# Decay tables in smaller portions, states' products a step later, values a step later with four buffers, new rows transposed twelve steps later: one layer of a hybrid transformer

## The chip, the core and the metric

The kernel runs on one core of one Trainium2 chip. The metric is the time of one execution on the device in microseconds (us); lower is better. PE is TensorE (matrix products and transposes), DVE VectorE, ACT ScalarE, POOL GpSimd, and SP the engine that issues most of the transfers.

## What is computed

One layer on a sequence of 2048 rows of width 1024, with 256 context rows beside it. Cut to what matters here:

```
h  = modulate(rmsnorm(x), sh1, sc1);  hc = modulate(rmsnorm(ctx), csh1, csc1)
rq, rk, rv, rg, aq, ak, av = split(h @ w_in)       # retention q, k, v, gate; attention q, k, v
log_gamma = log1p(-exp(ret_log_rate))
s_f = final state of the context's rk, rv          # and s_b, backward
ret = retention(rq, rk, rv, log_gamma, s_f) + the same backward, normed, gated with rg
att = softmax(q k^T / 8) v                         # 8 heads, 2 kv heads, keys of rows and context
x  = x + g1 * (concat(ret, att) @ w_out)
h2 = modulate(rmsnorm(x), sh2, sc2)
x  = x + g2 * (square(relu(h2 @ w_ff1)) @ w_ff2)
out = rmsnorm(x) * final_norm_g
```

Retention works in chunks of 128 rows: a state (128 x 128 for each of 4 heads) is multiplied by a decay and gets k^T v of the chunk added, with k weighted by powers of gamma. The decays come from `log_gamma`, by a series.

## The kernel before

The order of all work is written out by hand; nothing is rearranged by a scheduler. Each engine executes its own queue in that order, and semaphores make it wait for what it needs.

**Stage 1, to about 647 us: projections.** The rows stand in three groups of 6 tiles of 128 rows. For each group and each of six column groups of `w_in` (RK, AKV, AQ, RQ, RV, RG; 512 columns wide, AKV 256) there are six units, one for each tile. A unit is 24 matmuls (L1063 to L1065): eight slices of 128 of the width, in three products of high and low halves of fp32. A column group's weights come in four quarters: a transfer (L506, SP), the high half (L512, ACT), the low half (L516, DVE). All other work hangs on the unit's number: `do(s, part, fn)` puts `fn` behind the products of unit s, and `run_step` (L307) runs the parts in the order hi, evac, turned, low, vec, pool, root, aux, turn, load, store. The AKV column of the second group has units 30 to 35, AQ 36 to 41, RK 42 to 47, then RQ, RV, RG; of the third group AKV has 66 to 71, AQ 72 to 77, RK 78 to 83.

Three pieces of that other work are changed:

- `decay_tables(34)` (L936 to L1012) loads the rates; ACT makes u = exp(rate) in unit s + 2; DVE makes the series of log(1 - u) in s + 3 (22 instructions of 128x8, L955 to L967), ACT the plain logarithm in s + 4, DVE the choice between both in s + 5 (`choose`, 4 instructions, L974 to L977), four times two instructions of 128x128 in s + 6 (`power`, L982 and L983), ACT the exponentials in s + 7, DVE the diagonal in s + 8.
- `forward_state(45 + 3c, c)` (L1016 to L1052) for twelve chunks c: SP loads k and v (L1024) into two slots of 512 in the buffer `early`; POOL weighs k one unit later (L1027); PE makes four products of 128x128 a unit after that (L1032, tile psf; a row of the trace counts x8, since each is issued in two passes); DVE updates the state (L1038, L1040), and SP stores it (L1045).
- `value_parts(82)` (L751 on) loads the attention's values and splits them for the products.

Transposes of keys and queries stand in the units too (L744 for attention's keys, L618 for the others); they use a ring of two banks (psx), which DVE or ACT frees by a copy (L749, the keys' copy; L692).

**Stage 2, about 647 to 1612 us: attention, with retention and the output projection woven in.** `on(k, phase, fn)` puts work in step k; in a step the phases run in the order begin, scores, piece, maximum, early, exp, cast, low, chain, pe, values, late, dma. 32 groups (16 tiles of rows, 2 kv heads) have 18 steps each. A step holds for one key tile two score matmuls (L209, L210), and for the next group one piece (L172), a product whose maximum DVE takes (L185, nm) as the softmax's shift. Behind: exp (L215, ACT, into p32, a ring of three pairs of key tiles), cast to the high half phi (L219, ACT), the low half plo (L226 on POOL for the pairs 0, 2, 4, 6, 7; L228 on DVE for the others) and, every second step, `values` (L242, L243): 16 products of plo and phi with the values. `combine` (L261, POOL, tile ma) ends a group. `retention(24)` (from L1391) makes the backward states and the chunks' output in steps that follow one another every 35 (L1417: state products; L1441: scores). `output_weights(20)` loads the output weights, POOL scales them (L1555, wos), ACT and DVE split them (L1560). `output_tile` (L1568 to L1682) multiplies a finished tile with them: transposes of retention's and attention's rows (L1588), 16 places of products (L1603 to L1605), residual, sum of squares, `norm` on POOL (L1630, tile xr); then, at k + 27 and k + 28, `transpose_x` (L1635, PE, into a bank), one step later `modulate` (L1640, DVE, tile u) and `shift_` (L1645, POOL), and `store_h`. `h_pair` (L1686 to L1716) combines two such tiles on POOL for the feed-forward part, in steps that begin when the tile is finished (the step that `output_tile` returns). `more_keys` (L1306 to L1310) copies keys for the second kv head.

**Stage 3, to 2815 us: the feed-forward part**, by seven products in place of eight, then the last norm.

Of the kernel before, what the change touches and what calls it, by code (L numbers as in the profile page):

```python
# [13 lines left out]
F16 = mybir.dt.float16  # L14
# [3 lines left out]
ALU = mybir.AluOpType  # L18
# [4 lines left out]
P = 128  # L23
# [33 lines left out]
def layer_kernel(ctx: ExitStack, tc: tile.TileContext, a: dict, out: bass.AP):  # L57
# [89 lines left out]
    class Group:  # L147
# [69 lines left out]
        def cast(self, j):  # L217
            hi = self.hi[j] = pp.tile([P, 2, 512], F16, name="phi", tag="phi")
            nc.scalar.activation(hi, self.p[j], AF.Copy)  # L219

        def low(self, j, i=None):
            if i in (None, 0):
                self.lo[j] = pp.tile([P, 2, 512], F16, name="plo", tag="plo")
# [43 lines left out]
    with ExitStack() as st, tc.manual_schedule():  # L267
# [671 lines left out]
        def decay_tables(s):  # L939
# [15 lines left out]
            def series():  # L955
                u, w1, z, zz, lg = (x[v] for v in ("u", "w1", "z", "zz", "lg"))
                nc.vector.tensor_scalar(w1, u, -1.0, 1.0, op0=ALU.mult, op1=ALU.add)
                nc.vector.tensor_scalar(z, u, -1.0, 2.0, op0=ALU.mult, op1=ALU.add)
                nc.vector.reciprocal(z, z)
                nc.vector.tensor_mul(z, z, u)  # L960
                nc.vector.tensor_mul(zz, z, z)
                nc.vector.tensor_scalar(lg, zz, 1.0 / 17, 1.0 / 15, op0=ALU.mult, op1=ALU.add)
                for k in range(13, 0, -2):
                    nc.vector.tensor_mul(lg, lg, zz)
                    nc.vector.tensor_scalar_add(lg, lg, 1.0 / k)
                nc.vector.tensor_mul(lg, lg, z)
                nc.vector.tensor_scalar_mul(lg, lg, -2.0)  # L967
# [38 lines left out]
            do(s + 3, "aux", series)  # L1006
            do(s + 4, "hi", log)
            do(s + 5, "aux", choose)
            for h in range(4):
                do(s + 6, "aux", power, h)  # L1010
                do(s + 7, "hi", tables, h)
            do(s + 7, "hi", rest)  # L1012
            do(s + 8, "aux", diagonal)
# [3 lines left out]
        def forward_state(s, c):  # L1017

            k, v = (early[:, 512 * i : 512 * i + 512].rearrange("p (h d) -> p h d", h=4) for i in range(2))
            st = early[:, 1536:2048].rearrange("p (h d) -> p h d", h=4)  # L1020

            def load():
                for to, src in ((k, rk_d[c]), (v, rv_d[c])):
                    nc.sync.dma_start(to.rearrange("p h d -> p (h d)"), src)  # L1024
# [22 lines left out]
            do(s, "load", load)  # L1047
            do(s + 1, "pool", weigh)
            do(s + 2, "turn", product)
            do(s + 3, "vec", update)  # L1050
            if c > 0:
                do(s + 4, "store", keep_state)  # L1052
# [83 lines left out]
        value_parts(first[2, C_RK] + 4)  # L1136
        decay_tables(first[1, C_AKV] + 4)
# [1093 lines left out]
```

## Time and profile before

| | |
|---|---|
| median of 3 runs | 2817.0 us (2816.18 to 2820.16) |
| profiled execution: its time, its span | 2816.61 us, 2814.7 us |
| mean granted TensorE clock | 0.989 |
| bytes moved | 482.88 MB, 172 GB/s in the mean |
| share of the chain that ended last: PE, DVE, POOL | 57%, 6%, 5% |

The share of an engine is its busy time by the span. "PEld" is the loading of PE's stationary operand, which overlaps its products. In a list of waits, "PE o L242 <- POOL plo L226: 18.4, 15, 2.5" reads: before its line 242 (which writes tile o), PE waited for POOL's line 226 (which writes plo), 18.4 us in 15 waits, 2.5 the longest. In rows by time, the first two numbers are start and duration in us, then engine, line, operation, output and inputs, shapes; in brackets stands how long the engine was idle before it and for whom. Rows of windows give for each stretch its length and the busy time of each engine (with the number of instructions), the granted clock, the DMA engines' busy share and GB/s.

### The profile page before, as it was taken

How to read it: one execution, taken by the hardware profiler on the slowest of the kernel's cores; microseconds unless marked ns; L12 is line 12 of the kernel's file. 1: busy time of each engine (PE TensorE's matmuls, PEld its weight loads, DVE VectorE, ACT ScalarE, POOL GpSimd, SP SyncE). 2: the span in 40 equal slices, each digit the busy share in tenths (PEclk: the TensorE clock that was granted, in tenths of full speed). 3: DMA queues.
4: the chain of work that ended last, by engine and by line, in shares of the span. 5: the costliest groups of instructions: out<-in, count | busy, mean ns of one | idle time of the engine just before them, and what ended most of it. 6: DMA issues, size and time to landing. Idle time of an engine off the chain costs nothing.

```text
span 2814.7 us, 46065 instructions
## 1 busy us (share of the span) xinstructions
PE 2668.3 (95%) x16756; PEld 1602.8 (57%) x16756; DVE 2190.4 (78%) x3126; ACT 1465.0 (52%) x2441; POOL 1933.2 (69%) x1499
## 2 busy tenths in 40 slices
PE   6998999997899999999999899999999999999996
PEld 3877788875566566555666544444444444444443
DVE  3678847777977787877877578898876688888898
ACT  2535443335777777777777745555544322222232
POOL 2527427434766668886766679988865688888887
PEclk9999999999999999999999999999999999999998
DMA  6776876855211223333121264777783757575543
GB/s 213 269 260 203 283 274 218 283 180 184 66 52 52 66 72 106 96 105 91 60 82 45 91 236 138 234 252 248 245 275 106 249 180 284 176 274 171 187 143 112
DMA packets 329778, 482.88 MB, mean 172 GB/s; under 512 B 81991, under 2 KB 192839, under 8 KB 325070
## 3 DMA queue, kind: packets, MB, share of 16 engines
q1 hardware_dynamic: 329166, 479.66, 51.7%
q8 instruction: 132, 2.16, 0.3%
q14 instruction: 96, 0.79, 0.1%
q10 hardware_dynamic: 384, 0.26, 0.0%
HBM read 327.64 MB, written 152.20 MB: 170 GB/s over the span
## 4 chain that ended last, share of the span: by engine, by line
PE 57%; DVE 6%; POOL 5%; issue 2%; DMA 2%; ACT 1%; SPq 0%; POOLq 0%; DVEq 0%; ACTq 0%
PE pu L1838 7%; PE pu L1839 7%; PE pu L1837 7%; PE pd L2056 5%; PE pd L2054 5%; PE pd L2055 5%; PE o L243 3%; PE st L210 3%; PE st L209 3%; PE mp L172 3%; PE o L242 2%; PE bank L1603 2%; PE bank L1605 2%; PE bank L1604 2%; POOL plo L226 1%
## 5 line engine op out<-in xcount | busy, mean ns | idle before, releaser
L185 DVE TENSOR_REDUCE nm<-mp 128x1 f32<-128x512 f32 (+1 forms) x576 | 390.1, 684 | 170.9 <-PE mp L172 144.7
L226 POOL TENSOR_TENSOR plo<-p,phi 128x1024 f16<-128x1024 f32 x160 | 354.1, 2214 | 175.3 <-ACT phi L219 148.0
L215 ACT ACTIVATE p<-st 128x512 f32<-128x512 f32 x576 | 338.5, 597 | 196.8 <-PE st L210 128.2
L2056 PE MATMUL pd<-w,uf 128*128 128x512 f16 x896 | 339.6, 379 | 1.2 <-DVE uf L2047 1.2
L1837 PE MATMUL pu<-hf,w1f 128*128 128x512 f16 x896 | 339.6, 379 | 0.0
L1838 PE MATMUL pu<-hf,w1f 128*128 128x512 f16 x896 | 339.6, 379 | 0.0
L1839 PE MATMUL pu<-hf,w1f 128*128 128x512 f16 x896 | 339.6, 379 | 0.0
L2054 PE MATMUL pd<-w,uf 128*128 128x512 f16 x896 | 339.6, 379 | 0.0
L2055 PE MATMUL pd<-w,uf 128*128 128x512 f16 x896 | 339.6, 379 | 0.0
L219 ACT ACTIVATE phi<-p 128x1024 f16<-128x1024 f32 x288 | 303.9, 1055 | 0.0
L1065 PE MATMUL pso<-whi,hlo_l 128*128 128x512 f32 (+1 forms) x768 | 288.5, 376 | 10.6 <-DVE hlo_l L492 10.5
L1063 PE MATMUL pso<-whi,hhi_l 128*128 128x512 f32 (+1 forms) x768 | 297.5, 387 | 0.8 <-ACT whi L512 0.8
L1064 PE MATMUL pso<-wlo,hhi_l 128*128 128x512 f32 (+1 forms) x768 | 286.8, 373 | 0.8 <-DVE wlo L516 0.8
L242 PE MATMUL o<-wv,plo 128*128 128x65 f16 x2304 | 234.7, 193 | 25.2 <-POOL plo L226 18.4
L228 DVE TENSOR_TENSOR plo<-p,phi 128x512 f16<-128x512 f32 x256 | 241.2, 943 | 19.5 <-ACT phi L219 14.4
L2094 POOL TENSOR_TENSOR d<-d,g2b 128x512 f32<-128x512 f32 x126 | 199.8, 1586 | 70.5 <-DVE d L2066 68.6
L242 PEld LDWEIGHTS <-plo 128*128 128x128 f16 x2304 | 206.3, 98 | 68.6 <-POOL plo L226 26.4
L243 PE MATMUL o<-wv,phi 128*128 128x129 f16 x2304 | 242.5, 220 | 0.0
L1854 POOL TENSOR_TENSOR r<-r 128x512 f32<-128x512 f32 x128 | 172.1, 1350 | 86.4 <-ACT r L1853 86.1
L209 PE MATMUL st<-qr,ks 128*128 128x512 f16 x576 | 220.6, 383 | 7.0 <-ACT p L215 6.6
L210 PE MATMUL st<-qr,ks 128*128 128x512 f16 x576 | 220.7, 383 | 0.4
L172 PE MATMUL mp<-ks,qr 128*128 128x512 f16 x512 | 196.8, 384 | 25.6 <-DVE nm L185 25.2
(330 smaller groups left out, 6249.1 us busy)
## 6 DMA issues: line engine op xcount, KB each, us to landing
wm<-in_w_ff SPq DMA_DIRECT2D x64, 512.0 KB, 6.9
u<-r SPq DMA_DIRECT2D x128, 256.0 KB, 4.6
ur<-u SPq DMA_DIRECT2D x128, 256.0 KB, 5.9
y<-x SPq DMA_DIRECT2D x64, 512.0 KB, 6.4
wst<-in_w_in SPq DMA_DIRECT2D x60, 512.0 KB, 6.8
wf<-w2f SPq DMA_DIRECT2D x112, 256.0 KB, 3.9
w<-wf SPq DMA_DIRECT2D x28, 1024.0 KB, 10.1
w1r<-in_w_ff SPq DMA_DIRECT2D x48, 512.0 KB, 5.3
```

The source lines that it names most:

```text
L185: nc.vector.tensor_reduce(dst, src, axis=AX.X, op=ALU.max, negate=True)
L210: mm(ps, ks2[:, self.g, k], q[:, 1], start=False, stop=True)
L215: nc.scalar.activation(self.p[kt // 2][:, kt % 2], self.s.pop(kt), AF.Exp, scale=HD**-0.5)
L226: nc.gpsimd.tensor_tensor(lo, p, hi, op=ALU.subtract)
L242: mm(o[:, : HD + 1], lo[:, i, c], v[:, : HD + 1], start=False, stop=False)
L243: mm(o, hi[:, i, c], v[:, :VW], start=False, stop=last)
L1837: mm(pu[hf, i], whi, hi, start=k == 0, stop=False)
L1838: mm(pu[hf, i], whi, lo, start=False, stop=False)
L1839: mm(pu[hf, i], wlo, hi, start=False, stop=k == 3)
L2054: mm(ps, u[:, 0, b], w[:, b, 0], start=b == 0, stop=False)
L2055: mm(ps, u[:, 0, b], w[:, b, 1], start=False, stop=False)
L2056: mm(ps, u[:, 1, b], w[:, b, 0], start=False, stop=b == 3)
```

## The change

1. `phi` and `plo` get four buffers in place of three, `values` comes one step later (k + 2j + 7), a group's end likewise, and what follows attention (`prelude`) one step later.
2. The decay series runs in three portions in units s + 3 to s + 5, `choose` moves to s + 6, `power` to s + 7 and s + 8 (two heads each), the tables to s + 8 and s + 9, the diagonal to s + 10; the whole begins one unit later.
3. In `forward_state` the loads rotate over three slots; k is loaded one unit earlier, v in the same unit as before; the product comes two units behind the weighting in place of one, the update and the store follow. The slot of v for chunk c + 1 is that of k of chunk c, so that its load waits for the product of chunk c.
4. `value_parts` begins two units later.
5. `transpose_x` moves from k + 27 and k + 28 to k + 39 and k + 41 (not for tile 1 and the last one), and all that hangs on it with it: modulate, shift, stores, and the steps of `h_pair`.
6. `retention` begins four steps later, and `more_keys(1)` moves from steps 26, 30, 34 to 30, 33, 36.

```diff
--- before.py
+++ after.py
@@ -215,12 +215,12 @@
             nc.scalar.activation(self.p[kt // 2][:, kt % 2], self.s.pop(kt), AF.Exp, scale=HD**-0.5)
 
         def cast(self, j):
-            hi = self.hi[j] = pp.tile([P, 2, 512], F16, name="phi", tag="phi")
+            hi = self.hi[j] = pp.tile([P, 2, 512], F16, name="phi", tag="phi", bufs=4)
             nc.scalar.activation(hi, self.p[j], AF.Copy)
 
         def low(self, j, i=None):
             if i in (None, 0):
-                self.lo[j] = pp.tile([P, 2, 512], F16, name="plo", tag="plo")
+                self.lo[j] = pp.tile([P, 2, 512], F16, name="plo", tag="plo", bufs=4)
             lo, p, hi = self.lo[j], self.p[j], self.hi[j]
             if i is None:
                 nc.gpsimd.tensor_tensor(lo, p, hi, op=ALU.subtract)
@@ -952,19 +952,21 @@
             def base():
                 nc.scalar.activation(x["u"], x["lr"], AF.Exp)
 
-            def series():
+            def series(i):
                 u, w1, z, zz, lg = (x[v] for v in ("u", "w1", "z", "zz", "lg"))
-                nc.vector.tensor_scalar(w1, u, -1.0, 1.0, op0=ALU.mult, op1=ALU.add)
-                nc.vector.tensor_scalar(z, u, -1.0, 2.0, op0=ALU.mult, op1=ALU.add)
-                nc.vector.reciprocal(z, z)
-                nc.vector.tensor_mul(z, z, u)
-                nc.vector.tensor_mul(zz, z, z)
-                nc.vector.tensor_scalar(lg, zz, 1.0 / 17, 1.0 / 15, op0=ALU.mult, op1=ALU.add)
-                for k in range(13, 0, -2):
+                if i == 0:
+                    nc.vector.tensor_scalar(w1, u, -1.0, 1.0, op0=ALU.mult, op1=ALU.add)
+                    nc.vector.tensor_scalar(z, u, -1.0, 2.0, op0=ALU.mult, op1=ALU.add)
+                    nc.vector.reciprocal(z, z)
+                    nc.vector.tensor_mul(z, z, u)
+                    nc.vector.tensor_mul(zz, z, z)
+                    nc.vector.tensor_scalar(lg, zz, 1.0 / 17, 1.0 / 15, op0=ALU.mult, op1=ALU.add)
+                for k in ((13, 11), (9, 7, 5), (3, 1))[i]:
                     nc.vector.tensor_mul(lg, lg, zz)
                     nc.vector.tensor_scalar_add(lg, lg, 1.0 / k)
-                nc.vector.tensor_mul(lg, lg, z)
-                nc.vector.tensor_scalar_mul(lg, lg, -2.0)
+                if i == 2:
+                    nc.vector.tensor_mul(lg, lg, z)
+                    nc.vector.tensor_scalar_mul(lg, lg, -2.0)
 
             def log():
                 nc.scalar.activation(x["ln"], x["w1"], AF.Ln)
@@ -1003,25 +1005,27 @@
 
             do(s, "load", load)
             do(s + 2, "hi", base)
-            do(s + 3, "aux", series)
-            do(s + 4, "hi", log)
-            do(s + 5, "aux", choose)
+            for i in range(3):
+                do(s + 3 + i, "aux", series, i)
+            do(s + 5, "hi", log)
+            do(s + 6, "aux", choose)
             for h in range(4):
-                do(s + 6, "aux", power, h)
-                do(s + 7, "hi", tables, h)
-            do(s + 7, "hi", rest)
-            do(s + 8, "aux", diagonal)
+                do(s + 7 + h // 2, "aux", power, h)
+                do(s + 8 + h // 2, "hi", tables, h)
+            do(s + 8, "hi", rest)
+            do(s + 10, "aux", diagonal)
 
         states = {}
 
         def forward_state(s, c):
 
-            k, v = (early[:, 512 * i : 512 * i + 512].rearrange("p (h d) -> p h d", h=4) for i in range(2))
-            st = early[:, 1536:2048].rearrange("p (h d) -> p h d", h=4)
-
-            def load():
-                for to, src in ((k, rk_d[c]), (v, rv_d[c])):
-                    nc.sync.dma_start(to.rearrange("p h d -> p (h d)"), src)
+            k, v, st = (
+                early[:, 512 * i : 512 * i + 512].rearrange("p (h d) -> p h d", h=4)
+                for i in (2 * c % 3, (2 * c + 1) % 3, 3)
+            )
+
+            def load(to, src):
+                nc.sync.dma_start(to.rearrange("p h d -> p (h d)"), src)
 
             def weigh():
                 nc.gpsimd.tensor_tensor(k, k, bc(kd[:, 0].unsqueeze(2), [P, 4, P]), op=ALU.mult)
@@ -1044,12 +1048,13 @@
             def keep_state():
                 nc.sync.dma_start(sf_d[c - 1], st.rearrange("p h d -> p (h d)"))
 
-            do(s, "load", load)
+            do(s - 1 if c else s, "load", load, k, rk_d[c])
+            do(s, "load", load, v, rv_d[c])
             do(s + 1, "pool", weigh)
-            do(s + 2, "turn", product)
-            do(s + 3, "vec", update)
+            do(s + 3, "turn", product)
+            do(s + 4, "vec", update)
             if c > 0:
-                do(s + 4, "store", keep_state)
+                do(s + 5, "store", keep_state)
 
         AKV, AQ, RK, RV, RQ, RG = (
             (C_AKV, 256), (C_AQ, 512), (C_RK, 512), (C_RV, 512), (C_RQ, 512), (C_RG, 512)
@@ -1133,8 +1138,8 @@
         at += slots((1, C_RK, range(6)), (1, C_RQ, range(6)), (2, C_AQ, range(6)), (2, C_RK, range(3)))
         for i in range(32, 72):
             magnitude_of(i, at.pop(0))
-        value_parts(first[2, C_RK] + 4)
-        decay_tables(first[1, C_AKV] + 4)
+        value_parts(first[2, C_RK] + 6)
+        decay_tables(first[1, C_AKV] + 5)
         for c in range(STATES):
             forward_state(first[1, C_RK] + 3 + 3 * c, c)
         ff_scales(first[2, C_RV] - 3)
@@ -1369,12 +1374,12 @@
                 else:
                     for i in range(2):
                         on(k + 2 * j + 4 + i, "low", g.low, j, i)
-                on(k + 2 * j + 6, "values", g.values, j)
-            k += NK + 5
+                on(k + 2 * j + 7, "values", g.values, j)
+            k += NK + 6
             on(k, "cast", g.evacuate)
             on(k + 1, "chain", g.invert)
             on(k + 2, "late", g.combine, ats)
-        return NK * len(groups) + LAG + 8
+        return NK * len(groups) + LAG + 9
 
 
 
@@ -1672,7 +1677,7 @@
                 rest.extend([(f, q) for f in (transpose_x, modulate, shift_, store_h)])
             return made, made + 5
         for q in range(2):
-            at = k + (31 if t == 1 else 27) + q
+            at = k + (31 + q if t == 1 else 39 + 2 * q)
             on(at, "pe", transpose_x, q)
             on(at + 1, "early", modulate, q)
             on(at + 1, "late", shift_, q)
@@ -1718,9 +1723,9 @@
 
     for i in range(3):
         on(18 + i, "begin", more_keys, 0, i)
-        on(26 + 4 * i, "late", more_keys, 1, i)
+        on(30 + 3 * i, "late", more_keys, 1, i)
     done = attention()
-    retention(24)
+    retention(28)
     output_weights(20)
     for n, t in enumerate(range(NT - 1, -1, -1)):
         made_at, last = output_tile(t, R0 + 43 + RF * n, n == NT - 1)
```

The lines of the changed kernel are up to 5 higher (L1032 is L1036 there, L1635 is L1640). Three places in the order of instructions:

On DVE, around the keys' copy L749 that follows `power`, with the small instructions of the decay tables (tile early), the modulation's accumulation (macc) and the weights' low halves (wlo). Before:

```order
L378 SCALAR_TENSOR_TENSOR macc<-wmo,cc,macc 128x512 x2
L982 TENSOR_SCALAR early<-early 128x128
L983 SCALAR_TENSOR_TENSOR early<-early 128x128
...
L516 TENSOR_TENSOR wlo<-wst,whi 128x1024 x3
L749 CAST ks<-psx 128x2x128
L692 TENSOR_TENSOR qhl<-psx,qhl 128x512
```

And with the change:

```order
L378 SCALAR_TENSOR_TENSOR macc<-wmo,cc,macc 128x512 x2
L965 TENSOR_TENSOR early<-early 128x8
L966 TENSOR_SCALAR early<-early 128x8
...
L968 TENSOR_TENSOR early<-early 128x8
L969 TENSOR_SCALAR early<-early 128x8
L516 TENSOR_TENSOR wlo<-wst,whi 128x1024 x3
L749 CAST ks<-psx 128x2x128
L692 TENSOR_TENSOR qhl<-psx,qhl 128x512
```

Where four pairs of L982 and L983 on 128x128 stood ahead of the copy, the last three pairs of the series on 128x8 stand now; `choose` follows one unit later, and `power` in the two units behind that, ahead of copies of queries (L692).

On PE, at the eighth of the states' products (psf), with the units' products around it (pso; the numbers in hhi_l and hlo_l name the tile). Before:

```order
L1063 MATMUL pso<-whi,hhi_l_4449 128x256
L1064 MATMUL pso<-wlo,hhi_l_4449 128x256
L1065 MATMUL pso<-whi,hlo_l_4450 128x256
L1032 MATMUL psf<-early 128x128 x4
L1063 MATMUL pso<-whi,hhi_l_4509 128x256
L1064 MATMUL pso<-wlo,hhi_l_4509 128x256
```

And with the change:

```order
L1068 MATMUL pso<-whi,hhi_l_4509 128x256
L1069 MATMUL pso<-wlo,hhi_l_4509 128x256
L1070 MATMUL pso<-whi,hlo_l_4510 128x256
L1036 MATMUL psf<-early 128x128 x4
L1068 MATMUL pso<-whi,hhi_l_4571 128x256
L1069 MATMUL pso<-wlo,hhi_l_4571 128x256
```

The product stands one unit later, behind the products of tile 4509 instead of ahead of them.

On PE in attention, at the transposes of a tile's new rows (L1635 before, L1640 after; xr is the row tile that POOL's `norm` leaves), with scores (st), pieces (mp) and values (o) around. Before:

```order
L172 MATMUL mp<-ks,qr 128x512
L1441 MATMUL bank_9793<-oqt,okt 128x128 x4
L1635 MATMUL bank_9798<-ident,xr 128x128 x4
L209 LDWEIGHTS ks
L209 MATMUL st<-qr,ks 128x512
...
L1635 MATMUL bank_9815<-ident,xr 128x128 x4
L242 LDWEIGHTS plo
L242 MATMUL o_9440<-wv,plo 128x65
```

And with the change:

```order
L209 MATMUL st<-qr,ks 128x512
L210 LDWEIGHTS ks_6684
L210 MATMUL st<-qr,ks_6684 128x512
L196 MATMUL mp<-ident,mt_6691 128x128 x4
L172 LDWEIGHTS qr
L172 MATMUL mp<-ks,qr 128x512
L1640 MATMUL bank_10084<-ident,xr 128x128 x4
L242 LDWEIGHTS plo
L242 MATMUL o_9875<-wv,plo 128x65
```

Before, the two halves of a tile stood in neighbouring steps, the first beside a retention score product; now each stands in a step with values, twelve and thirteen steps later.

## Prediction

> **What bounds the kernel now.** I read the profile from the whole to the place: busy shares, then stretches, then who waits for whom, then the rows at each wait that the change touches.
>
> ```profile
> span 2814.7 us, 46065 instructions
> PE 2668.3 (95%) x16756; PEld 1602.8 (57%) x16756; DVE 2190.4 (78%) x3126; ACT 1465.0 (52%) x2441; POOL 1933.2 (69%) x1499
> ```
>
> ```profile
> core 0: us, PE busy (x) PEld busy (x) DVE busy (x) ACT busy (x) POOL busy (x), PEclk, DMA share, GB/s
> 0.00:640.00 640.00, 599.11 (x3065) 481.74 (x3066) 446.53 (x753) 260.16 (x465) 289.24 (x335) 0.99 0.71 241
> 640.00:780.00 140.00, 109.02 (x943) 74.42 (x942) 120.44 (x191) 91.25 (x146) 88.37 (x59) 0.94 0.39 121
> 780.00:1610.00 830.00, 781.96 (x7283) 511.89 (x7282) 634.09 (x1103) 631.97 (x1035) 573.55 (x428) 0.99 0.25 74
> 1610.00:2770.00 1160.00, 1154.68 (x5369) 524.79 (x5367) 952.67 (x1038) 469.83 (x769) 951.47 (x651) 1.00 0.64 213
> ```
>
> TensorE (PE) is busy 95% of the span. The change leaves its work as it is (the same products and transposes), so it can only return or add idle time. The feed-forward stretch (1610 to 2770) has 5 us of idle PE and nothing of the change in it but its entrance; projections, retention and attention have 41, 31 and 48 us. Whom PE waits for there, in the list of waits (total, times, longest, in us):
>
> ```profile
> PE mp L172 <- DVE nm L185: 25.2, 34, 2.2
> PE o L242 <- POOL plo L226: 18.4, 15, 2.5
> PE bank L1635 <- POOL xr L1630: 7.1, 8, 2.4
> PE o L242 <- DVE plo L228: 6.7, 11, 1.8
> PE st L209 <- ACT p L215: 6.6, 8, 3.4
> PE psx L744 <- DVE ks L749: 6.4, 2, 6.0
> PE psx L618 <- DVE ks L749: 1.0, 1, 1.0
> PE bank L1588 <- DVE u L1640: 3.9, 10, 0.8
> PE bank L1588 <- POOL ma L261: 2.9, 1, 2.9
> PE bank L1635 <- DVE u L1640: 1.1, 2, 0.7
> ```
>
> Each part of the change meets one of these rows, or one of three waits shown below. So the question for each is what becomes late next. I work with the profiled execution, which took 2816.61 us (1.9 outside its span); the median of the three runs is 0.4 above it.
>
> **A. Decay tables in smaller portions.** On VectorE (DVE) around 280 us:
>
> ```profile
> 268.44 0.17 DVE L974 TENSOR_SCALAR early<-early 128x8 f32<-128x8 f32 x1
> 269.01 1.22 DVE L516 TENSOR_TENSOR wlo<-wst,whi 128x1024 fp32r<-128x1024 f32 x1
> 275.86 0.28 DVE L982 TENSOR_SCALAR early<-early 128x128 f32<-128x128 f32 x1
> 279.49 3.49 DVE L516 TENSOR_TENSOR wlo<-wst,whi 128x1024 fp32r<-128x1024 f32 x3
> 282.90 0.42 DVE L749 CAST ks<-psx 128x256 f16<-128x256 f32 x1
> 283.46 0.66 PE L744 MATMUL psx<-ident,kn 128*128 128x128 f32 x2 [6.00 <-DVE ks L749]
> 284.80 0.78 PE L1063 MATMUL pso<-whi,hhi_l 128*128 128x512 f32 x1
> 286.76 0.39 PE L1065 MATMUL pso<-whi,hlo_l 128*128 128x512 f32 x1
> ```
>
> PE waits 6.00 us for L749, the copy that frees a transposes' bank; DVE comes to it at 282.90, out of a backlog. Ahead of it the change takes out the eight instructions of `power` (275.86 to 279.49: 3.63 us) and the four of `choose` (268.44 to 269.01: 0.57), which go one step later, `power` in two portions. The 22 small instructions of the series (0.17 us each by the first row, 3.7 in all) stay ahead, in three portions. So L749 comes 3.63 + 0.57 = **4.2 us** earlier, less than the 6.00, and all of it is PE's gain if the moved portions meet no wait in the units behind, where the list names none of theirs. Bounds: 0 (the series' portions or `power` delay the next copy) and 7.0 (the 6.00, and 1.0 that a transpose of L618 waits for the same line).
>
> Does the clock come back too? The matmul at 284.80 takes 0.78 us and that at 286.76 takes 0.39, so a few behind the wait ran slowly, about 1.2 us together. The wait that stays is about 2 us, and waits of about that length were followed by a lower clock elsewhere (2.77 us at 453, 2.53 at 1159):
>
> ```profile
> 450.00:460.00 10.00, 7.24 (x48) 7.03 (x47) 8.49 (x17) 4.28 (x10) 9.51 (x13) 0.83 0.47 143
> 1160.00:1170.00 10.00, 9.70 (x77) 7.13 (x76) 5.85 (x9) 6.36 (x10) 10.00 (x8) 0.83 0.30 74
> ```
>
> I count no clock gain. [...]
>
> **B. States' products two steps behind the weighting.**
>
> ```profile
> 453.04 1.57 PE L1032 MATMUL psf<-early 128*128 128x128 f32 x8 [2.77 <-POOL early L1027]
> 458.98 0.60 SPq L506 DMA_DIRECT2D wst<-in_w_in  x1
> 464.20 1.05 PE L1032 MATMUL psf<-early 128*128 128x128 f32 x8
> 465.78 1.41 DVE L516 TENSOR_TENSOR wlo<-wst,whi 128x1024 fp32r<-128x1024 f32 x1 [1.22 <-ACT whi L512]
> ```
>
> One product of twelve waits, 2.77 us, in the narrow column: the two products stand three narrow units apart, 11.2 us with the first, so a narrow unit is 3.2 us and a wide one 6.4. A step later POOL has long weighted, and the wait goes. Late next is the last quarter of the following column's weights: its low halves are ready at 465.78 + 1.41 = 467.2. PE needs them 18 of 24 matmuls (4.0 us at 0.22, the distance of full-speed matmuls in the rows under D) into the unit that starts at 464.20 + 1.05 = 465.2, at 469.2. PE can come 2.0 us earlier before it waits there. The product of 464.20, which moves out of the stretch ahead and comes one unit later, uses 1.0 of that without being a gain: **1.0 us**. Bounds: 0, and 2.77 with about 1.5 of slow matmuls, 4.3.
>
> **C. Start of retention and attention.**
>
> ```profile
> 659.43 0.68 PE L1417 MATMUL bank<-orv,okw 128*128 128x128 f32 x4 [2.35 <-DMA orv<-rv]
> 661.07 1.26 POOL L1555 TENSOR_TENSOR wos<-wos,g1b 128x512 f32<-128x512 f32 x1 [1.91 <-DMA wos<-in_w_out]
> 662.36 0.63 ACT L1560 ACTIVATE wo<-wos 128x512 f16<-128x512 f32 x1 [6.55 <-POOL wos L1555]
> 663.53 0.58 PE L209 MATMUL st<-qr,ks 128*128 128x512 f16 x1 [3.42 <-ACT p L215]
> ```
>
> PE waits 2.35 us for a retention load and 3.42 behind an exponential that stands on ScalarE behind the output weights. With retention four steps later, its loads no longer share SP's queue with the first output weights. The two waits, 5.8 us, are the upper bound. But DVE is busy 120 of the 140 us of this stretch, and the postponed portions (scores, products, their splits) come back four steps later, into it. Lower bound 0; nearest the row of DVE: **2 us**.
>
> **D. Attention to 1610.** A step holds two score matmuls and a piece:
>
> ```profile
> 1151.40 0.60 ACT L215 ACTIVATE p<-st 128x512 f32<-128x512 f32 x1 [1.28 <-POOL plo L226]
> 1151.42 0.20 PE L242 MATMUL o<-wv,plo 128*128 128x65 f16 x1 [1.86 <-POOL plo L226]
> 1152.13 0.38 PE L209 MATMUL st<-qr,ks 128*128 128x512 f16 x1
> 1152.78 0.38 PE L209 MATMUL st<-qr,ks 128*128 128x512 f16 x1
> ```
>
> 1152.13 to 1152.78 is one such step, 0.65 us. `values` one step later gives each plo at least this much more. The waits for plo are 18.4 us in 15 (POOL) and 6.7 in 11 (DVE), 25.1 in 26; at 0.65 each the gain is at most 26 x 0.65 = 16.9. Where POOL is late for several pairs in a row, though, the slack is gained once, and at 1151.40 ScalarE waits for the same plo, through the three p32 buffers, which do not grow: scores would wait in its place. I take half of 16.9, **8**. The fourth phi and plo buffers are needed to hold a pair a step longer and cost no instruction.
>
> The new rows' transposes wait 7.1 us for `norm` on POOL, and 3.9 + 1.1 more go on banks that wait for `modulate` (u). Twelve steps later the 7.1 go nearly all. The modulate, shift, two stores and the h_pair steps that hang on the tile's end move by 13 steps and are no fewer; POOL's `shift` and splits then stand beside other pairs' plo, which they delay in turn. Of the 12.1 us I take **4.5**. Together 12.5; upper bound 25.1 + 12.1 = 37, lower bound 4 (the 7.1 with 3 of it returned as waits for plo).
>
> **At nothing, and one loss.** `value_parts` two units later: its DVE and ACT work fills units in which PE waits for none of it (it has no row in the list). `more_keys` 4, 3 and 2 steps later has its reader, the scores of the last key tiles, many steps behind. Attention ends a step later; the last tile's transposes already wait 2.9 us for its `combine` (ma), one step's 0.65 is added at most: **-0.5**.
>
> **Sum.** 4.2 + 1.0 + 2 + 12.5 - 0.5 = 19.2 us; 2816.6 - 19.2 = 2797.4; by the median, 0.4 above, 2797.8, so 2798.
>
> **Rivals.**
>
> *All the named waits go.* 7.0 + 4.3 + 5.8 + 37 - 0.5 = 53.6, with a little slow clock left: about 2765. For it: every part meets a wait that is in the list. Against: POOL at 69% and DVE at 76 to 86% come in bursts, and a later reader does not make them faster.
>
> *The engines set the pace.* In attention PE's largest wait is not touched: 25.2 us in 34 for DVE's maxima (L172). If DVE and POOL decide, PE arrives earlier and waits longer there and at L209, and what is left is 4.2 of A and 1 of the rest: about 2812, half of the cases on either side of a change of 0.2% (5.6 us), which is about what a measurement of this kernel can tell from none.
>
> *Slower: SP is held.* In the states' part, SP waits for products before it may load the next chunk:
>
> ```profile
> SPq L1024 <- PE psf L1032: 48.0, 6, 14.1
> ```
>
> The new v load waits for a product one unit later, and everything behind it in SP's queue with it: the x tiles, the rows' stores and, in five columns, a quarter of the next weights. That is up to 6.4 us in four wide columns and 3.2 in the narrow one, 28.8 in all. It decides from the point at which a quarter comes late: from issue (458.98) to low halves (467.2) are 8.2 us, and four issues ahead of it, at 0.60, make about 2.4 (estimate): 10.6. PE needs it 2.75 units after the product, 17.6 us in wide columns and 2 x 3.2 + 4.8 = 11.2 in the narrow one. A margin of 7 and of 0.6: if bursts of transfers (DMA 0.71 busy in this stage) eat it in all five, the time is 2816.6 - 19.2 + 28.8 = 2826.
>
> **How the numbers follow.** Forecast 0.55 (2798; its own range 2785 to 2810), all waits go 0.12 (2765, from 2755 to 2785), engines set the pace 0.21 (2812), SP held 0.12 (2826). The range 2772 to 2817 takes in the forecast, the pace and about half of the first rival; about 0.18 is left out. Faster by over 0.2%: 0.55 + 0.12 + half of 0.21 = 0.77; within: the other half and a share of SP's case that is made up by the rest, 0.12; slower: 0.11.
>
> **What would show it.** A: the wait behind L749's copy at 2 us, not 6. B: no wait of a states' product, and no wait for weights' low halves just behind 465. C: no wait for orv, DVE still full from 700 to 760. D: waits for plo about halved, none for xr, and the row L172 for DVE not above 30 us; if that row, or L209's, grows by 10, the second rival is right. SP: its waits for states' products grow by tens of us in any case; if PE then waits for wlo or whi, the third is. The forecast is most easily wrong in D, whose bounds lie 33 us apart.

## The result and the profile after

The changed kernel takes 2811.55 us in the median of 17 runs (2806.72 to 2814.77), the kernel before 2818.35 beside it (2816.18 to 2820.33): a ratio of 0.9975, 95% interval 0.9968 to 0.9982. That is 6.8 us faster, a third of the 19 forecast; the time lies inside the range. The page of the changed kernel, from one of its longer executions (2814.71 us):

```profile
span 2812.9 us, 46058 instructions
PE 2665.1 (95%) x16756; PEld 1604.4 (57%) x16756; DVE 2196.2 (78%) x3126; ACT 1455.2 (52%) x2441; POOL 1928.0 (69%) x1499
```

The stretches, columns as before:

```profile
0.00:640.00 640.00, 590.87 (x3007) 473.88 (x3008) 442.33 (x730) 256.50 (x458) 284.71 (x331) 0.98 0.71 239
640.00:780.00 140.00, 109.04 (x911) 76.58 (x910) 116.40 (x201) 88.61 (x143) 87.15 (x61) 0.96 0.42 132
780.00:1610.00 830.00, 788.68 (x7396) 520.85 (x7395) 650.12 (x1121) 629.82 (x1048) 575.02 (x432) 0.99 0.26 75
```

PE does 6.7 us more in 780 to 1610, and 8.2 less in the first 640. The stages' ends say the same: the last product of the projections starts at 646.7 us before and at 659.1 now (12.4 later; 3.9 of that are there already at 145 us, ahead of every edit), and from the first to the last score matmul (L209) it is 955.9 us before and 940.1 now (15.8 shorter). **The sum forecast for attention came in, and the projections lost more than half of it again.** What PE waits for now:

```profile
PE mp L172 <- DVE nm L185: 27.4, 36, 2.2
PE st L209 <- ACT p L215: 19.3, 27, 4.4
PE mp L196 <- DVE mt L191: 8.1, 8, 1.7
PE o L242 <- POOL plo L226: 7.9, 5, 3.6
PE psx L744 <- DVE ks L749: 5.8, 2, 4.5
PE pso L1069 <- DVE wlo L516: 5.8, 4, 3.3
PE psx L618 <- DVE ks L749: 2.3, 1, 2.3
```

The waits for xr and for the states' weighted keys are gone, those for plo fell from 25.1 to 7.9. But L209's grew from 6.6 to 19.3, L744's hardly fell, and one for the weights' low halves (wlo), 0.8 before, is 5.8 now.

### The profile page after: what moved, and what is told of

The parts are those of the page before. It is cut to its first block, busy times and chain, and to the rows that moved or that the text cites. A ratio compares the mean times of both kernels' runs of the same rounds, so it can differ in the third digit from the quotient of the medians.

```text
span 2812.9 us, 46058 instructions
## 1 busy us (share of the span) xinstructions
PE 2665.1 (95%) x16756; PEld 1604.4 (57%) x16756; DVE 2196.2 (78%) x3126; ACT 1455.2 (52%) x2441; POOL 1928.0 (69%) x1499
## 3 DMA queue, kind: packets, MB, share of 16 engines
q8 instruction: 132, 2.16, 0.3%
## 4 chain that ended last, share of the span: by engine, by line
PE 57%; DVE 7%; POOL 3%; DMA 2%; issue 2%; ACT 2%; SPq 0%; POOLq 0%; DVEq 0%; ACTq 0%
PE pu L1843 7%; PE pu L1844 7%; PE pu L1842 7%; PE pd L2061 5%; PE pd L2059 5%; PE pd L2060 5%; PE o L243 3%; PE st L209 3%; PE st L210 3%; PE mp L172 3%; DVE plo L228 2%; PE bank L1610 2%; PE bank L1609 2%; PE bank L1608 2%; DVE nm L185 2%; PE o L242 2%
## 5 line engine op out<-in xcount | busy, mean ns | idle before, releaser
L228 DVE TENSOR_TENSOR plo<-p,phi 128x512 f16<-128x512 f32 x256 | 245.7, 961 | 17.2 <-ACT phi L219 15.8
L209 PE MATMUL st<-qr,ks 128*128 128x512 f16 x576 | 219.7, 381 | 20.3 <-ACT p L215 19.3
```

## The experiments

Eighteen kernels, each timed beside the kernel before. A kernel's difference is from the median of before that was timed with it. Since the projections run up to 6 us later in one profile than in another at 140 us, ahead of any edit, I compare distances in them: a, from the last but one of the second group's key transposes (L744) to the last, around the wait at 283; b, from there to the second-last new tile's transposes near 440.

### Which part lost: projections against attention

Theory 1: the decay tables' portions cost time behind 290. Theory 2: SP is held by the states' loads (the slower rival). Theory 3: chance.

The decay alone (point 2 of the change on the kernel before):

```diff
-            do(s + 3, "aux", series)
+            for i in range(3):
+                do(s + 3 + i, "aux", series, i)
...
-                do(s + 6, "aux", power, h)
+                do(s + 7 + h // 2, "aux", power, h)
...
-        decay_tables(first[1, C_AKV] + 4)
+        decay_tables(first[1, C_AKV] + 5)
```

> Only the decay tables in portions. Theory 1 (the tables on ACT now stand ahead of the queries' copies and wait for DVE's power, so DVE and ACT take turns in waiting and the next weights come late): 4 to 9 us slower than before, about 2824, with idle DVE behind ACT qhl near 300 and a wait of PE for wlo near 330. Theory 2 (the states' loads hold SP; the decay's term of the prediction holds): 4 us faster, about 2814. Theory 3 (stage 1 differs by chance between runs): within 2 us of before.

2820.81 us, ratio 1.0010 (1.0001 to 1.0019): slower, not 4.2 faster, though by less than the 4 to 9 us of theory 1.

The states' part alone (points 3 and 4):

```diff
-            do(s + 2, "turn", product)
-            do(s + 3, "vec", update)
+            do(s + 3, "turn", product)
+            do(s + 4, "vec", update)
```

> Only the states' products a unit later, with three slots and value_parts two units later. Theory 1: 1 us faster, 2817. Theory 2: 5 to 9 us slower, about 2825, with waits of PE for wlo or whi behind 330. Theory 3: within 2 us of before.

2819.46 us, 1.0001 (0.9992 to 1.0009): nothing that can be told from no change, although SP's waits for the states' products are 69.6 us in it (48.0 before). Of the 5 to 9 us of theory 2 nothing is seen.

Attention's edits alone (points 1, 5 and 6; the stage of projections as before):

```diff
-                on(k + 2 * j + 6, "values", g.values, j)
+                on(k + 2 * j + 7, "values", g.values, j)
...
-            at = k + (31 if t == 1 else 27) + q
+            at = k + (31 + q if t == 1 else 39 + 2 * q)
...
-    retention(24)
+    retention(28)
```

> Only the edits of attention (values with four buffers, new rows' transposes, retention and more_keys). Theories 1 and 2 (the loss lies in stage 1): 14 to 16 us faster than before, about 2803. Theory 3 (attention gains less than its profile shows): 7 us faster, about 2811.

2802.60 us, 0.9941 (0.9929 to 0.9954): 16 us faster.

All but the decay (the changed kernel with point 2 taken back):

```diff
-        decay_tables(first[1, C_AKV] + 5)
+        decay_tables(first[1, C_AKV] + 4)
```

(and its portions as before.)

> The changed kernel with the decay tables as before. Theory 1: 5 to 9 us faster than the changed kernel, about 2803. Theory 2: 4 us slower than the changed kernel, about 2815. Theory 3: like the changed kernel, 2811.

2807.17 us, 0.9950 (0.9937 to 0.9964): 14 us faster than before, where the changed kernel is 7; the two intervals lie apart. Theory 1 holds for the sign, theory 3 falls; the sum of the parts (+2.1, +0.8, -16.1: 2805) is not reached by the changed kernel. The next kernels ask why.

All but the states' part, and the changed kernel again:

```diff
-        value_parts(first[2, C_RK] + 6)
+        value_parts(first[2, C_RK] + 4)
```

(and loads, slots and products as before.)

> The changed kernel with the states' part (products, slots, value_parts) as before. If the parts add up (decay 2.1 slower, states 0.8 slower, attention 16.1 faster, as the first four runs have it): 0.8 us faster than the changed kernel's repeat, about 2805 to 2811. If decay and states disturb each other: 4 us faster than it or more.

> The changed kernel itself, beside the other three. If the parts add up: 2805, by the sum of the first runs. If decay and states disturb each other, or the chance of a run decides several us: 2811, as measured first.

2808.21 (0.9961, 0.9949 to 0.9973) and 2814.04 (0.9978, 0.9968 to 0.9988). By the medians decay and states cost more together than apart; the intervals overlap, so the time doesn't show it.

v loaded a unit later:

```diff
-            do(s, "load", load, v, rv_d[c])
+            do(s + 1, "load", load, v, rv_d[c])
```

> The changed kernel with the load of v one unit later, so that SP has no product ahead of it to wait for in its own unit. Theory 2 (SP is held): SP's waits for psf fall from tens of us to a few, and the time falls by 2 to 5 us. Theory 1: SP's waits fall alike, the time stays within 1 us.

SP's waits for the states' products, of the changed kernel and of this one:

```profile
SPq L1028 <- PE psf L1036: 67.9, 9, 16.0
```

```profile
SPq L1028 <- PE psf L1036: 32.0, 6, 9.1
```

They halve, and the time is 2811.45 (0.9974, 0.9963 to 0.9984): 2.6 us below the changed kernel timed with it by the medians, 1.1 by the ratios, and the intervals overlap. This kernel alone doesn't decide against the 2 to 5 us of theory 2; PE's wait for wlo behind 330 is 3.27 us in it as in the changed kernel, and the states' part alone lost nothing.

### How the decay's portions lose

In the changed kernel DVE, then PE, around the wait that was to shrink by 4.2 us:

```profile
263.05 1.90 DVE L378 SCALAR_TENSOR_TENSOR macc<-wmo,cc,macc 128x512 f32<-128x512 f32 x2 [1.38 <-DMA wmo<-in_w_mod]
282.03 4.56 DVE L516 TENSOR_TENSOR wlo<-wst,whi 128x1024 fp32r<-128x1024 f32 x3
286.52 0.41 DVE L749 CAST ks<-psx 128x256 f16<-128x256 f32 x1
287.08 0.66 PE L744 MATMUL psx<-ident,kn 128*128 128x128 f32 x2 [4.45 <-DVE ks L749]
```

The backlog was not solid. Before, the series (255 to 259) stood where DVE's next accumulation had no data yet; without it DVE waits 1.38 us for that transfer, and does the series' instructions later, ahead of the copy. The three low halves take 4.56 us here, 3.49 before. And the wait that shrinks from 6.00 to 4.45 comes back in part at the transposes ahead of it (L618 for the same line: 1.0 before, 2.3 now). Of 4.2 us some 0.3 are left: a is 13.5 before and 13.2 now.

Behind it, on ACT, DVE, SP and PE:

```profile
299.40 0.31 ACT L992 ACTIVATE dT<-early 128x128 f32<-128x128 f32 x1 [6.43 <-DVE early L985]
302.83 0.69 DVE L692 TENSOR_TENSOR qhl<-psx,qhl 128x512 f16<-128x512 f32 x1 [2.40 <-ACT qhl L689]
319.37 0.69 SPq L696 DMA_DIRECT2D aq<-qhl  x1
327.40 0.60 ACT L689 ACTIVATE qhl<-psx 128x512 f16<-128x512 f32 x1 [10.95 <-DMA aq<-qhl]
333.71 3.49 DVE L516 TENSOR_TENSOR wlo<-wst,whi 128x1024 fp32r<-128x1024 f32 x3
334.98 0.80 PE L1069 MATMUL pso<-wlo,hhi_l 128*128 128x512 f32 x1 [3.27 <-DVE wlo L516]
335.58 0.63 PE L1070 MATMUL pso<-whi,hlo_l 128*128 128x512 f32 x1
```

The exponentials of the tables stand on ACT ahead of the queries' copies (L689). They wait 6.43 us for the first portion's `power`, and DVE, which needs that copy, 2.40 us for ACT (and 1.93 for the next copy, behind the second portion). SP stands meanwhile at a load whose buffer DVE has to free (its waits of this kind between 300 and 340):

```profile
SPq L628 <- DVE t L546: 13.8, 3, 6.3
```

So the store of the second split comes at 319.37, and the next copy but one waits for the end of that transfer, until 327.40: the split has two buffers. The weights' high halves stand behind it on ACT, the low halves behind those on DVE, and PE waits 3.27 us. The matmuls behind take 0.63 and follow each other by 0.43 instead of 0.23, a dozen of them: 2.5 us more. The trace shows this order of events; the following kernels test it.

The changed kernel with the tables a unit later:

```diff
-                do(s + 8 + h // 2, "hi", tables, h)
-            do(s + 8, "hi", rest)
-            do(s + 10, "aux", diagonal)
+                do(s + 9 + h // 2, "hi", tables, h)
+            do(s + 9, "hi", rest)
+            do(s + 11, "aux", diagonal)
```

> The changed kernel with ACT's exponentials of the decay tables, and the diagonal, one unit later, so that DVE's power has a whole unit before ACT asks for it. Theory 1 (ACT stands at the tables and with it the queries' copies behind them; DVE, SP's stores and the next weights follow): the idle time of DVE behind ACT qhl near 302 and 311 goes, and with it PE's waits for ys near 329 and for wlo near 334: 5 us faster than the changed kernel. Rival 1b (DVE is late by the portions themselves, whatever ACT does): the two waits of PE stay, time within 1 us of the changed kernel.

2808.38 us, 0.9961 (0.9948 to 0.9974), 5.7 below the changed kernel timed with it by the medians and 4.8 by the ratios, whose intervals overlap a little. DVE no longer waits for ACT near 300 and PE's wait for ys (the queries that the transposes L618 read; 1.2 us near 329 in the changed kernel) is gone, but not that for wlo:

```profile
320.53 0.60 ACT L689 ACTIVATE qhl<-psx 128x512 f16<-128x512 f32 x1 [9.25 <-DMA aq<-qhl]
328.91 0.80 PE L1069 MATMUL pso<-wlo,hhi_l 128*128 128x512 f32 x1 [3.23 <-DVE wlo L516]
```

So the tables' place is part of the loss, that wait for ys. The rest of what b gains here (3.8 us, in the table below) lies in slow matmuls, 6 behind the wait for wlo where the changed kernel has 14, and fewer behind the one at 283. That the end of the transfer decides the wait for wlo is read from the rows; no kernel changes it by itself. Next, on attention's edits: the series in portions with `power` whole, and `power` in halves with the series whole.

```diff
+            for i in range(3):
+                do(s + 3 + i, "aux", series, i)
...
+                do(s + 7, "aux", power, h)
+                do(s + 8, "hi", tables, h)
```

> Attention's edits, with the series in three portions, and choose, power (in one piece), tables and diagonal one unit later than before; the whole begins where it began before. Theory 1 as it stands now (what was ahead of the third series portion, in time in which DVE was behind anyway, comes back ahead of the queries' copies, which SP's stores and the next weights follow; above all power and the tables, which ACT has to wait for): power in one piece one unit later makes L749's wait near 283 shorter by up to 4 us and brings a wait for wlo near 330, 2 to 4 us slower than attention's edits alone (2805 to 2807). Rival 1c (the later start of the tables is what costs, not the portions): within 1 us of attention's edits alone, or up to 3 faster.

```diff
+                do(s + 6 + h // 2, "aux", power, h)
+                do(s + 7 + h // 2, "hi", tables, h)
```

> Attention's edits, with the series and choose as before and power in two portions, the second of them, its tables and the diagonal one unit later. Theory 1: half of power leaves the place ahead of L749, 1.8 us less of its wait near 283, and the second tables delay one copy of queries: 1 us faster to 2 us slower than attention's edits alone. Rival 1c: 2 us faster.

2805.05 (0.9945, 0.9933 to 0.9958) and 2805.41 (0.9947, 0.9935 to 0.9960): neither can be told from attention's edits alone (0.9941), and by the time the first fits rival 1c (within 1 us) as well as theory 1. The traces tell them apart: the first has a shorter wait at 283 (3.4) and a wait for wlo of 2.2, as theory 1 said; the second has none, so halving `power` does not bring it. Whether the portions of the series bring it or the later `power` and tables behind them stays open.

Last, the undivided tables twelve units earlier, on attention's edits:

```diff
-        decay_tables(first[1, C_AKV] + 4)
+        decay_tables(first[1, C_AKV] - 8)
```

> Attention's edits, with the decay tables undivided as before, but 12 units earlier, where DVE is busy 5 to 7 of every 10 us (170 to 220) and not 9.6 to 9.9 (260 to 310). Theory 1 (DVE's backlog from 260 to 335 is what counts; portions inside it only move the loss): PE's wait for L749 near 283 falls from 6.0 to below 2, none comes near 330, 4 to 6 us faster than attention's edits alone, about 2797. Rival 1d (DVE's order there hangs on the modulation's weights, L376 and L378, which wait for their transfers anyway): the wait stays at 4 us or more, within 2 us of attention's edits alone.

2799.99 us, 0.9930 (0.9918 to 0.9942): the lowest median of all, 19 us faster than before and, by the ratios, 3 faster than attention's edits alone. That is less than the 4 to 6 expected, and the intervals overlap, so the time doesn't show this last gain; the profile does. The wait is gone, and none comes near 330. PE, then the stretch 250 to 340 of this kernel, of before, and of the changed one:

```profile
282.56 0.41 PE L744 MATMUL psx<-ident,kn 128*128 128x128 f32 x2 [0.41 <-DVE ks L749]
```

```profile
250.00:340.00 90.00, 89.40 (x416) 71.28 (x415) 77.12 (x113) 38.67 (x69) 56.23 (x61) 1.00 0.89 302
```

```profile
250.00:340.00 90.00, 82.97 (x380) 65.75 (x379) 80.66 (x138) 43.53 (x83) 50.57 (x52) 0.96 0.83 280
```

```profile
250.00:340.00 90.00, 78.81 (x337) 61.97 (x336) 73.85 (x132) 42.30 (x82) 47.84 (x53) 0.93 0.77 258
```

PE works 89.40 of 90 us, against 82.97 and 78.81. (DVE pays a part back earlier: PE waits 1.4 us for x_l, a tile to transpose, at 230, and from the first group's last key transposes to the second's last but one it takes 3.1 us more.) The distances:

| kernel | a, us | b, us |
|---|---|---|
| before | 13.5 | 155.2 |
| states only; all but decay; attention only | 13.2; 13.4; 13.3 | 156.6; 156.5; 156.7 |
| the seven kernels of the next part, projections as before | 11.7 to 13.5 | 155.2 to 156.8 |
| decay only; all but states | 12.6; 13.9 | 161.4; 160.5 |
| changed; again; v later | 13.2; 13.4; 11.5 | 164.5; 164.6; 163.3 |
| changed, tables later | 11.1 | 160.7 |
| attention and series; and power halves | 11.5; 12.5 | 158.2; 155.7 |
| attention, decay early | 6.7 | 154.1 |

With the projections as before, a varies by 2 us from one profile to the next and b by 1.6. So the decay's portions gain nothing in a that can be told from chance, and lose 4 to 6 us in b without the states' part, 7 to 9 with it. PE's waits are 4.1 us of that in the decay alone (ys 1.73, wlo 2.35) and 4.5 in the changed kernel (1.20 and 3.27). The rest is slow matmuls, and their number changes from profile to profile behind waits of one length: 6, 9, 13 and 14 behind the wait for wlo of 3.23 to 3.27 us. Why the states' edits lengthen that wait by 0.9 was not found; the v load is not it (3.27 stays with it later).

### Where attention's 16 us come from

The prediction added up terms for values (8), the new rows (4.5) and retention (2). All eight combinations of the three:

> Only values one step later with four buffers. By the prediction's terms: 8 us faster than before, 2810; PE's waits for plo about halved, those for xr as before. Rival (the engines set the pace; PE waits for scores' exponentials in place of plo): 2 to 4 us faster, 2815.

> Only the new rows' transposes and what hangs on them 12 steps later. By the prediction's terms: 4.5 us faster than before, 2814; the waits for xr go, and some of them return as waits for plo. Rival (all of the 12.1 us go): 2806.

> Values a step later with four buffers, and the new rows' transposes 12 steps later; retention as before. Theory P (the two need each other: what PE no longer waits for at one reader it waits for at the other, and only both together free it): 10 us faster than before, about 2809. Theory R (the later start of retention makes the rest possible): 2 us faster at most, 2817.

> Only retention four steps later, with more_keys moved. Theory P: the 5 us that the stretch 640 to 780 lost in the profile of all of attention's edits, 2814. Theory R: 5 us there and as much behind it, 2809.

> Values and retention, new rows as before. Theory P: waits for xr stay at 7 to 13 us, 4 us faster than before, 2815. Theory R: 12 us faster, 2807.

> New rows and retention, values as before. Theory P: waits for plo at 25 us or above, 4 us faster than before, 2815. Theory R: 10 us faster, 2809.

Their edits are the pieces of the diff of attention's edits above, one or two at a time (values with its buffers, retention with more_keys). Scores: from the first to the last L209 in the profile. The waits are PE's in the stretch 640 to 1620.

| edits | us | ratio (95%) | scores, us | waits plo, xr and u, p, us |
|---|---|---|---|---|
| none | | 1 | 955.9 | 25.1, 11.6, 6.6 |
| values | 2821.33 | 1.0009 (1.0000 to 1.0018) | 956.5 | 3.2, 20.4, 20.7 |
| rows | 2822.84 | 1.0012 (1.0003 to 1.0021) | 960.5 | 38.3, 0.2, 6.4 |
| retention | 2817.93 | 1.0000 (0.9991 to 1.0009) | 957.0 | 25.2, 11.3, 5.8 |
| values, rows | 2810.47 | 0.9970 (0.9961 to 0.9979) | 945.6 | 7.9, 0, 19.0 |
| values, retention | 2814.22 | 0.9988 (0.9980 to 0.9997) | 947.9 | 3.2, 21.3, 18.9 |
| rows, retention | 2822.80 | 1.0015 (1.0006 to 1.0024) | 961.0 | 37.3, 0.2, 7.1 |
| all three | 2802.60 | 0.9941 (0.9929 to 0.9954) | 939.5 | 8.0, 0, 17.6 |

No edit gains alone. In the list of waits of "values" alone, PE waits at xr and at the scores for what it no longer waits for at plo:

```profile
PE st L209 <- ACT p L215: 20.7, 27, 3.3
PE bank L1635 <- POOL xr L1630: 12.8, 8, 3.8
PE o L242 <- POOL plo L226: 3.2, 1, 3.2
```

And of "rows" alone, at plo for what is gone at xr:

```profile
PE o L242 <- POOL plo L226: 30.0, 20, 5.1
PE o L242 <- DVE plo L228: 8.3, 12, 1.8
```

Theory P holds for the pair (8 us where each alone has none), but it also expected 5 us of retention alone and 4 of rows with retention, which did not come. Theory R does not hold, since the pair gains without retention, and retention alone is worth nothing. By the ratios retention's later start is worth 6 us beside values and 8 beside both, which neither theory had; why it needs values was not found.

The prediction named the ring of three p32 buffers as the reason why scores would wait instead. With rows and retention as changed, values and its buffers as before, and a fourth p32 buffer:

```diff
-                self.p[kt // 2] = pp.tile([P, 2, 512], F32, name="p32", tag="p32")
+                self.p[kt // 2] = pp.tile([P, 2, 512], F32, name="p32", tag="p32", bufs=4)
```

> New rows and retention as changed, values at their old step with three phi and plo buffers, and a fourth p32 buffer in their place. If the ring of p32 is what ties ACT to plo, and ACT's exponentials tie PE: ACT's waits for plo (48 us in the profile before) fall by more than half, and the time by 4 us or more against new rows with retention (2823). If the time of plo itself decides (POOL's and DVE's): PE's waits for plo stay near 37 us and the time within 2 us of 2823.

ACT's waits in 780 to 1610, of rows with retention, and of this kernel:

```profile
ACT p L215 <- PE st L210: 118.3, 207, 3.9
ACT p L215 <- DVE plo L228: 31.9, 18, 4.3
ACT p L215 <- POOL plo L226: 18.9, 15, 3.6
```

```profile
ACT p L215 <- PE st L210: 166.3, 240, 6.5
```

ACT waits for plo no more, and PE's waits for it are as long as before (38.2 us); 2819.88 us (1.0004, 0.9996 to 1.0013), by the ratios 3 below rows with retention, between the two expectations and with overlapping intervals. So with values at the old step the ring is not what makes PE wait for plo; that leaves POOL's and DVE's time for it. With values at the later step no kernel tried a larger ring.

## Why the prediction was right and wrong

- **What bounds the kernel**: right in that only PE's idle time was at stake, and that the feed-forward stretch stayed (1154.8 of 1160 us busy).
- **A, decay tables: the sign was wrong, and this is where the forecast failed.** 4.2 us were to be gained; 2.1 were lost by the part alone, and about 7 beside the other parts (0.9950 without the decay's portions, 0.9975 with them). Without them the other terms, 15.0 us in sum, met 14. The step that failed is "all of it is PE's gain if the moved portions meet no wait in the units behind, where the list names none of theirs". In those units DVE was full before:

```profile
290.00:300.00 10.00, 10.00 (x47) 7.49 (x46) 9.79 (x16) 3.72 (x7) 6.84 (x9) 1.00 0.90 298
300.00:310.00 10.00, 10.00 (x48) 8.21 (x47) 9.79 (x14) 4.55 (x8) 6.93 (x6) 1.00 0.51 149
```

  That a list shows no wait in units in which DVE is busy 9.8 of 10 us says that there is no slack left, not that there is room. The portions met the queries' copies, the split's two buffers and the next weights: 4.1 to 4.5 us of new waits of PE, and slow matmuls behind them. The other half, that L749 comes earlier by what is taken out ahead of it, failed too: DVE waits for a transfer where the series had stood (1.38 us), and other instructions run longer (the three low halves 4.56 us, 3.49 before).
- **The clock in A**: not counted, and none came back: the wait was 4.45 us, not the 2 it was reckoned with, and eleven matmuls ran slowly behind it where before three did. The prediction went by the length of the wait. The profiles show that between 2 and 3 us the length does not settle it. The same wait for hlo_l (the low half of a tile of rows), where no instruction of PE or DVE has been moved yet, before and in the decay alone:

```profile
238.96 0.38 PE L1065 MATMUL pso<-whi,hlo_l 128*128 128x256 f32 x1 [2.07 <-DVE hlo_l L492]
239.18 0.28 PE L1063 MATMUL pso<-whi,hhi_l 128*128 128x256 f32 x1
239.30 0.28 PE L1064 MATMUL pso<-wlo,hhi_l 128*128 128x256 f32 x1
```

```profile
239.74 0.58 PE L1068 MATMUL pso<-whi,hlo_l 128*128 128x256 f32 x1 [2.07 <-DVE hlo_l L492]
240.12 0.41 PE L1066 MATMUL pso<-whi,hhi_l 128*128 128x256 f32 x1
240.33 0.41 PE L1067 MATMUL pso<-wlo,hhi_l 128*128 128x256 f32 x1
```

  2.07 us both times; the matmuls behind follow each other by 0.12 us in one and by 0.21 in the other, for 3 us (granted clock 1.00 and 0.70 over the five us). And two rows of the decay alone stand against the changed kernel's 0.80 and 0.63 at the same place:

```profile
333.10 0.50 PE L1067 MATMUL pso<-wlo,hhi_l 128*128 128x512 f32 x1 [2.35 <-DVE wlo L516]
333.44 0.40 PE L1068 MATMUL pso<-whi,hlo_l 128*128 128x512 f32 x1
```

  Behind that wait the clock fell in all four profiles with 3.23 to 3.27 us (granted 0.66 to 0.91 over 330 to 340) and in none of the three with 2.16 to 2.35 (1.00), but by the rows above the shorter one could have slowed it too. Waits of 2.07, 2.77 and 3.27 us were followed by slow matmuls here, and waits of 2.07 and 2.77 in other profiles were not. Why one length has both outcomes was not shown; no run here tests it.
- **B, states' products**: right in which wait goes and what is late next, wrong in the room ahead of it. The 2.77 us wait is gone, and PE waits near 475 for the weights instead (1.03, 0.37 and 0.76 us in three places, 2.2 in all), where the prediction counted 2.0 us of room and said that no wait for low halves would come. Forecast 1.0, measured between 2.3 faster and 2.5 slower by the part's interval, which also takes in `value_parts`.
- **C, the start**: the wait for orv (2.35) is gone, as said; that behind the exponential (3.42) is not, it is 4.42 now. In the profile of attention's edits the scores are 3.9 us ahead after five groups, but retention alone is worth nothing by its end. It is not a term of its own: its worth came only beside values.
- **D, attention**: the sum was near (C, D and the tail 14.0, measured 16), the terms were wrong. Values was given 8 and the rows 4.5, each for itself; alone they give none. That PE's waits for plo, xr and p come from the same engines' bursts is how I read the table, in which the waits of an edit alone move and hardly shrink in sum. What the prediction's second rival said, that waits move, is what happens to each edit alone. Its sign was a poor one: L209's waits were to grow by 10 us if the rival was right; they grew by 12.7, and attention was 15.8 us shorter all the same.
- **The slower rival**: SP's waits grew from 48.0 to 67.9 us, as it said, and cost nothing that the times can tell.
- The pace rival's time, 2812, was hit by chance: not the engines' pace in attention held the gain back but a loss in the projections.

## What to carry to other kernels

Waits for the same engines need not be additive: here, with waits for POOL and DVE, moving one reader moved the wait to the next, and only with values and new rows moved together did the time fall by 8 us. Try such edits together before dropping them singly, and those of different stages apart, since one stage's gain can hide another's loss (16 gained, 9 lost here). Work that is late on a full engine can be moved to where the engine has slack: here, 12 units earlier, it took the wait of 6 us away (by the profile; the 3 us of time lie within the intervals), while dealing it out among units without slack brought new ones.

## What else the runs showed of the hardware

Behind waits of one length, between 2 and 3 us, the granted clock fell in some profiles and stayed in others. The wait for hlo_l near 240, 2.05 to 2.08 us in all twenty profiles, was followed by a granted clock below 1 in nine of them; the wait of a states' product near 455, 2.75 to 2.79 us in fourteen profiles, in eleven (2.77 us before and in attention and series, then 0.83 and 1.00 over 450 to 460); of PE's 53 waits of 3.2 us or more after the first 100 us of all profiles, 52 were (0.71 over 330 to 340 with the 3.27 us of the changed kernel; behind 3.22 us at 1152 in values and retention the score matmuls kept their 0.38). So part of what two profiles differ by is this, whatever the edit, and a single pair of rows says little about which wait is followed by a lower clock.

Three low halves of weights on DVE (128x1024) took 3.49 us before and 4.56 in the changed kernel, at the same place of the program: 1.22 each where POOL had nothing to do, and 1.77, 1.74 and 1.21 where POOL worked beside the first two (L550 and L553, to 284.4). In these two profiles no low half of that size without POOL's work beside it took over 1.26 us; with it some took 1.21 all the same, and the longest 2.10. That POOL is the cause was not tested by a kernel of its own.
